# Row sums of a 32 x 512 x 1024 tensor: another assignment of rows to partitions, larger loads, another division of the work, and another tail

## The chip, the cores and the metric

The kernel runs on one core of a Trainium2 chip. The metric is the device time of one execution in microseconds (us). Every run here is fast, that is undisturbed, with a granted clock of 1.0 (the full speed). The span that the profile shows is about 1.8 us shorter than the time of the same execution. The groups of runs were taken on different chips, each group with runs of the kernel before beside it, so across groups the ratios are safer to compare than the times.

## The reference

```python
x: float32 [32, 512, 1024]          # 67.1 MB
reference(x) = np.sum(x, axis=-1)   # float32 [32, 512], 64 KB
```

A load is issued from the queue of one engine (SyncE, ScalarE or GpSimd) and is carried by 16 DMA engines in packets. In the records here a packet is one contiguous run for one partition: a 4 MB load of the kernel before is 128 packets of 32 KB.

The input is read once and one addition is made per element. So this is a question of how long the loads take, and of what is left to do before the first and after the last byte.

## The kernel before

The 16384 rows are cut into 16 tiles of 1024 rows. Each tile is one contiguous block of 4 MB. Partition p gets 8 consecutive rows of it, a run of 32 KB, so neighbouring partitions lie 32 KB apart in HBM. VectorE sums the even tiles with one instruction each, ScalarE the odd ones row by row. Results go out in nine stores, eight of them from the GpSimd queue.

```python
Q = 8; W = Q * dim
x_t = x.flatten_outer_dims().rearrange("(n p q) d -> n p (q d)", p=P, q=Q, n=ntiles)
out_v = out.rearrange("b s -> (b s)").rearrange("(n p q) -> p n q", p=P, q=Q, n=ntiles)
bounds = list(range(2, ntiles - 1, 2)) + [ntiles - 1, ntiles]
head_launchers = [nc.sync, nc.scalar] * 6
...
for i in range(ntiles):
    t = inpool.tile([P, W], fp32)                 # 5 buffers of 4 MB
    if i >= ntiles - 2:                           # last two tiles: four loads of 2 rows each
        ...  # last tile: nc.vector.tensor_reduce of 128 x 2 x 1024, four times
    elif i % 2 == 0:
        eng.dma_start(out=t, in_=x_t[i])
        nc.vector.tensor_reduce(out=dst, in_=t.rearrange("p (q d) -> p q d", q=Q), ...)
    else:
        ...  # nc.scalar.activation(Copy, accum_out=dst[:, q:q+1]), 8 rows
    if (i + 1) in bounds:
        ...  # a store of the finished sums: nc.gpsimd, the last one nc.sync
```

## Time and profile before

Time before: 165.77 us (three runs, 165.76 to 165.94). In the trace:

| | us |
|---|---|
| first load packet starts | 1.75 |
| last load packet ends | 159.03 |
| last reduction starts, ends | 159.47, 161.76 |
| last store issued, span ends | 161.78, 164.15 |

The page of the kernel before, parts 1 and 2: busy share of each compute engine, then the span in 40 slices with the busy tenths of the DMA engines and the bytes they moved.

```profile
DVE 74.5 (45%) x13; ACT 64.3 (39%) x121; POOL 5.9 (4%) x12
DMA  7899999998999989999999899999999998999960
GB/s 256 383 479 415 407 479 391 447 449 383 503 391 439 457 384 471 423 407 479 391 441 455 385 471 415 409 479 399 439 447 391 472 417 383 421 423 419 423 243 1
```

No compute engine is half busy, while the DMA engines are busy from the first slice to the last but one. The chain that ended last and the table of windows agree. The window columns are start and end, length, VectorE, ScalarE and GpSimd busy time (with instructions), clock, DMA share, GB/s.

```profile
DMA 86%; DVE 7%; ACT 5%; issue 0%; ACTq 0%; SPq 0%
...
40.00:80.00 40.00, 24.91 (x3) 16.85 (x32) 1.45 (x2) 1.00 1.00 429
80.00:120.00 40.00, 18.52 (x3) 11.12 (x21) 0.73 (x1) 1.00 1.00 432
```

The timeline shows what comes after the stream. Columns are start, length, engine, line, operation, and in brackets the idle time before it and what ended it.

```profile
159.47 2.29 DVE L59 TENSOR_REDUCE stage<-t 128x2 f32<-128x2048 f32 x1 [0.21 <-DMA t<-in_x_dram]
161.78 0.35 SPq L99 DMA_DIRECT2D out_dram<-stage  x1
```

The trace also has a record of every DMA packet. A 32 KB packet takes 1213 ns and an 8 KB packet 311 ns. Sixteen engines at one 32 KB packet per 1213 ns are 432 GB/s. The Trainium skill, "DMA: Bandwidth & Descriptors", section "Where 436 GB/s comes from", puts the ceiling of the SBUF ports at 435 GB/s. This trace stays just below it: its middle windows run at 429 to 432.

### The profile page before, as it was taken

To read this page: it belongs to the slowest core of one execution; us is meant where nothing else is said; L and a number is where in the kernel's file an instruction comes from. 1 tells how busy PE (TensorE), PEld (TensorE's weight loads), DVE (VectorE), ACT (ScalarE), POOL (GpSimd) and SP (SyncE) were. 2 spreads that over 40 slices of the span, in tenths; PEclk is the share of its full clock that TensorE was granted. 3 is DMA by queue.
4 is the path that set the end of the run, shared out by engine and by line. 5 is a ranking of instruction groups with operands and counts; after the bars stand their busy time and mean duration, and the time that the engine had idled before them with its cause. 6 is when DMAs were issued, how large, how long until landed. Compare 5 with 4: busy or idle time off the path is not lost.

```text
span 164.1 us, 241 instructions
## 1 busy us (share of the span) xinstructions
DVE 74.5 (45%) x13; ACT 64.3 (39%) x121; POOL 5.9 (4%) x12
## 2 busy tenths in 40 slices
DVE  0000049600794990039700892595008920055994
ACT  3000049600693000099101980000496006999940
POOL 0000000200001000000100001000001000010110
DMA  7899999998999989999999899999999998999960
GB/s 256 383 479 415 407 479 391 447 449 383 503 391 439 457 384 471 423 407 479 391 441 455 385 471 415 409 479 399 439 447 391 472 417 383 421 423 419 423 243 1
DMA packets 3569, 67.18 MB, mean 409 GB/s; under 512 B 640, under 2 KB 752, under 8 KB 752
## 3 DMA queue, kind: packets, MB, share of 16 engines
q1 hardware_dynamic: 2448, 41.95, 60.1%
q10 hardware_dynamic: 864, 25.17, 35.5%
q0 software_dynamic: 256, 0.06, 0.2%
q14 instruction: 1, 0.01, 0.0%
HBM read 67.11 MB, written 0.07 MB: 409 GB/s over the span
## 4 chain that ended last, share of the span: by engine, by line
DMA 86%; DVE 7%; ACT 5%; issue 0%; ACTq 0%; SPq 0%
DMA t<-in_x_dram 86%; DVE stage L78 5%; ACT sc L88 5%; DVE stage L59 1%; ACTq L85 0%; SPq L77 0%; SPq L85 0%; ACTq L88 0%
## 5 line engine op out<-in xcount | busy, mean ns | idle before, releaser
L88 ACT ACTIVATE sc<-t 128x1024 f32<-128x1024 f32 x56 | 58.3, 1041 | 91.7 <-DMA t<-in_x_dram 91.7
L78 DVE TENSOR_REDUCE stage<-t 128x8 f32<-128x8192 f32 x7 | 60.8, 8686 | 71.6 <-DMA t<-in_x_dram 71.6
L59 DVE TENSOR_REDUCE stage<-t 128x2 f32<-128x2048 f32 x6 | 13.7, 2286 | 15.6 <-DMA t<-in_x_dram 15.6
L99 POOL DMA_DIRECT2D out_dram<-stage x8 | 5.7, 718 | 152.3 <-ACT sc L88 98.8
L88 ACT ACTIVATION_READ_ACCUMULATOR sc<-t 128x1 f32 x56 | 10.4, 186 | 0.0
L70 ACT ACTIVATE sc<-t 128x1024 f32<-128x1024 f32 x4 | 4.2, 1039 | 0.0
L88 ACT ACT_TABLE_LOAD x1 | 1.3, 1283 | 1.7 <-PEq L114 1.7
L70 ACT ACTIVATION_READ_ACCUMULATOR sc<-t 128x1 f32 x4 | 0.7, 185 | 0.0
L114 POOL MEMSET const-float32-0.0<- 128x1 f32 x1 | 0.1, 99 | 0.2 <-issue 0.2
L114 POOL MEMSET const-bfloat16-1.0<- 128x1 bf16 x1 | 0.1, 102 | 0.0
L114 POOL MEMSET const-float32-1.0<- 128x1 f32 x1 | 0.1, 99 | 0.0
L114 POOL MEMSET const-uint8-127<- 128x1 uint8 x1 | 0.1, 99 | 0.0
## 6 DMA issues: line engine op xcount, KB each, us to landing
t<-in_x_dram SPq DMA_DIRECT2D x8, 4096.0 KB, 39.8
t<-in_x_dram ACTq DMA_DIRECT2D x6, 4096.0 KB, 31.0
t<-in_x_dram SPq DMA_DIRECT2D x8, 1024.0 KB, 27.5
out_dram<-stage POOLq DMA_DIRECT2D x7, 8.0 KB, 8.0
out_dram<-stage POOLq DMA_DIRECT2D x1, 4.0 KB, 1.7
out_dram<-stage SPq DMA_DIRECT2D x1, 4.0 KB, 1.4
```

The lines of the kernel that those rows point to most:

```text
L59: nc.vector.tensor_reduce(out=sdst, in_=t[:, s * QS * dim : (s + 1) * QS * dim].rearrange("p (q d) -> p q d", q=QS), axis=mybir.AxisListTy ...
L70: nc.scalar.activation(out=sc, in_=t[:, q * dim : (q + 1) * dim], func=mybir.ActivationFunctionType.Copy, accum_out=dst[:, q : q + 1],)
L78: nc.vector.tensor_reduce(out=dst, in_=t.rearrange("p (q d) -> p q d", q=Q), axis=mybir.AxisListType.X, op=mybir.AluOpType.add,)
L88: nc.scalar.activation(out=sc, in_=t[:, q * dim : (q + 1) * dim], func=mybir.ActivationFunctionType.Copy, accum_out=dst[:, q : q + 1],)
L99: oeng.dma_start(out=out_v[:, n0:n1], in_=src)
L114: nc = _bacc.Bacc("TRN2", target_bir_lowering=False, num_devices=1)
```

## The change

The intent: give each partition 128 consecutive rows, so that loads are 64 KB runs and the whole result is one store of 512 B per partition; issue everything from one queue; let VectorE do the bulk; and let the last pieces fall in size (8, 4, 2, 1 rows, then three cuts of one row) so that little work is left when the last byte lands.

```diff
-    x_t = x.flatten_outer_dims().rearrange("(n p q) d -> n p (q d)", p=P, q=Q, n=ntiles)
-    out_v = out.rearrange("b s -> (b s)").rearrange("(n p q) -> p n q", p=P, q=Q, n=ntiles)
+    J = rows // P                                   # 128
+    BIG = 16
+    x_v = x.flatten_outer_dims().rearrange("(p j) d -> p j d", p=P)
+    out_v = out.rearrange("b s -> (b s)").rearrange("(p j) -> p j", p=P)
+    nbig = J // BIG - 1                             # 7
+    tail = [(8, 4), (4, 2), (2, 1)]                 # rows, of which ScalarE takes
...
+        def rows_of(t, a, n, j, n_act):
+            nv = n - n_act
+            block = t[:, a * dim : (a + n) * dim].rearrange("p (n d) -> p n d", d=dim)
+            nc.sync.dma_start(out=block, in_=x_v[:, j : j + n, :])
+            if nv:
+                vec(sums[:, j : j + nv], block[:, :nv, :])
+            for q in range(nv, n):
+                act(sums[:, j + q : j + q + 1], block[:, q, :], dim)
+        for i in range(nbig):
+            t = inpool.tile([P, BIG * dim + 2], fp32)     # 3 buffers of 8 MB
+            rows_of(t, 0, BIG, i * BIG, BIG // 2 if i == nbig - 1 else 0)
+        t = inpool.tile([P, BIG * dim + 2], fp32)
+        a = 0
+        for n, n_act in tail:
+            rows_of(t, a, n, nbig * BIG + a, n_act)
+            a += n
+        rows_of(t, a, 1, nbig * BIG + a, 1)
...
+        cuts = [0, 384, 768, dim]
+        for c0, c1 in zip(cuts, cuts[1:]):
+            nc.sync.dma_start(out=last[:, c0:c1], in_=x_v[:, j, c0:c1])
+        for i, (c0, c1) in enumerate(zip(cuts, cuts[1:])):
+            if c1 < dim:
+                vec(last[:, dim + i : dim + i + 1], last[:, c0:c1])
+            else:
+                vec(sums[:, j : j + 1], last[:, c0 : dim + i])
+        nc.sync.dma_start(out=out_v, in_=sums)
```

With this row order neighbouring partitions lie 512 KB apart in HBM. That is the pitch.

More of the change, by code (lines that the diff above doesn't have):

```diff
@@ L17 @@
     fp32 = mybir.dt.float32
+    P = 128
     batch, seq, dim = x.shape
     rows = batch * seq
-    P = 128
-    Q = 8
-    W = Q * dim
-    ntiles = rows // (P * Q)
-    x_t = x.flatten_outer_dims().rearrange("(n p q) d -> n p (q d)", p=P, q=Q, n=ntiles)
-    out_v = out.rearrange("b s -> (b s)").rearrange("(n p q) -> p n q", p=P, q=Q, n=ntiles)
-    bounds = list(range(2, ntiles - 1, 2)) + [ntiles - 1, ntiles]
-    head_launchers = [nc.sync, nc.scalar] * 6
+    J = rows // P
+    BIG = 16
+    x_v = x.flatten_outer_dims().rearrange("(p j) d -> p j d", p=P)
@@ L33 @@
+    out_v = out.rearrange("b s -> (b s)").rearrange("(p j) -> p j", p=P)
+    nbig = J // BIG - 1
+    tail = [(8, 4), (4, 2), (2, 1)]
     with (
-        tc.tile_pool(name="in", bufs=5) as inpool,
-        tc.tile_pool(name="scratch", bufs=4) as spool,
+        tc.tile_pool(name="in", bufs=3) as inpool,
+        tc.tile_pool(name="scratch", bufs=1) as spool,
         tc.tile_pool(name="stage", bufs=1) as stpool,
     ):
-        stage = stpool.tile([P, ntiles * Q], fp32)
-        prev = 0
-        for i in range(ntiles):
-            t = inpool.tile([P, W], fp32)
-            eng = head_launchers[i] if i < len(head_launchers) else nc.sync
-            dst = stage[:, i * Q : (i + 1) * Q]
-            if i >= ntiles - 2:
-                NSUB = 4
-                QS = Q // NSUB
-                engs = (
-                    ["s", "v", "s", "v"] if i == ntiles - 2 else ["v", "v", "v", "v"]
-                )
-                for s in range(NSUB):
-                    nc.sync.dma_start(
-                        out=t[:, s * QS * dim : (s + 1) * QS * dim],
-                        in_=x_t[i][:, s * QS * dim : (s + 1) * QS * dim],
-                    )
-                for s in range(NSUB):
-                    sdst = dst[:, s * QS : (s + 1) * QS]
-                    if engs[s] == "v":
-                        nc.vector.tensor_reduce(
-                            out=sdst,
-                            in_=t[:, s * QS * dim : (s + 1) * QS * dim].rearrange(
-                                "p (q d) -> p q d", q=QS
-                            ),
-                            axis=mybir.AxisListType.X,
-                            op=mybir.AluOpType.add,
-                        )
-                    else:
-                        for q in range(s * QS, (s + 1) * QS):
-                            sc = spool.tile([P, dim], fp32)
-                            nc.scalar.activation(
-                                out=sc,
-                                in_=t[:, q * dim : (q + 1) * dim],
-                                func=mybir.ActivationFunctionType.Copy,
-                                accum_out=dst[:, q : q + 1],
-                            )
-            elif i % 2 == 0:
-                eng.dma_start(out=t, in_=x_t[i])
-                nc.vector.tensor_reduce(
-                    out=dst,
-                    in_=t.rearrange("p (q d) -> p q d", q=Q),
-                    axis=mybir.AxisListType.X,
-                    op=mybir.AluOpType.add,
-                )
-            else:
-                eng.dma_start(out=t, in_=x_t[i])
-                for q in range(Q):
-                    sc = spool.tile([P, dim], fp32)
-                    nc.scalar.activation(
-                        out=sc,
-                        in_=t[:, q * dim : (q + 1) * dim],
-                        func=mybir.ActivationFunctionType.Copy,
-                        accum_out=dst[:, q : q + 1],
-                    )
-            if (i + 1) in bounds:
-                n0, n1 = prev, i + 1
-                prev = i + 1
-                src = stage[:, n0 * Q : n1 * Q].rearrange("p (n q) -> p n q", q=Q)
-                oeng = nc.sync if n1 == ntiles else nc.gpsimd
-                oeng.dma_start(out=out_v[:, n0:n1], in_=src)
@@ new lines, with vec, act @@
+        sums = stpool.tile([P, J], fp32)
+        scratch = spool.tile([P, dim], fp32)
+        def vec(dst, src):
+            nc.vector.tensor_reduce(
+                out=dst, in_=src, axis=mybir.AxisListType.X, op=mybir.AluOpType.add
+            )
+        def act(dst, src, n):
+            nc.scalar.activation(
+                out=scratch[:, :n],
+                in_=src,
+                func=mybir.ActivationFunctionType.Copy,
+                accum_out=dst,
+            )
+        def rows_of(t, a, n, j, n_act):
[6 more added lines that the diff above has]
+                act(sums[:, j + q : j + q + 1], block[:, q, :], dim)
@@ new lines @@
+        for i in range(nbig):
[7 more added lines that the diff above has]
+        rows_of(t, a, 1, nbig * BIG + a, 1)
+        a += 1
+        j = nbig * BIG + a
+        last = t[:, a * dim :]
+        cuts = [0, 384, 768, dim]
+        for c0, c1 in zip(cuts, cuts[1:]):
+            nc.sync.dma_start(out=last[:, c0:c1], in_=x_v[:, j, c0:c1])
```

## The prediction

> **What bounds the kernel now.** The loads. The page's part 2 shows the DMA engines at 9 tenths in nearly every slice, and the table of windows shows DMA share 1.00 and 429 to 432 GB/s from 40 to 120 us, while VectorE is busy 45% and ScalarE 39% of the 164.1 us span. The chain of waits that ended last is 86% load. By the trace's packet records loads run from 1.75 to 159.03 us; the single engines finish between 158.0 and 159.03. A 32 KB packet takes 1213 ns (27.0 GB/s, times 16 = 432), an 8 KB packet 311 ns. From the two I estimate 9 ns per packet plus 0.0367 ns per byte: 435.5 GB/s without packet cost. That is the 435 GB/s fabric ceiling in the Trainium skill, "DMA: Bandwidth & Descriptors", section "Where 436 GB/s comes from". So the steady stream has under 1% to give.
>
> After it (chain, timeline): a 2.29 us reduction of 128x2048 from 159.47, store issued at 161.78, end of span 164.15.
>
> **What the change does.**
> 1. Bulk in 64 KB runs: half as many packets. Estimate: 56 fewer per engine at 9 ns, 0.5 us off the stream (0 if the hardware cuts them into 32 KB again).
> 2. The eight GpSimd stores go: 128 packets of about 28 ns and 128 semaphore writes of 9 ns on 16 engines, 0.3 us off the stream (queue 0: 0.2% of engine time).
> 3. The last reduction shrinks from 2048 to 258 elements per partition. From 8686 ns for 8192 and 2286 for 2048 (1.04 to 1.06 ns per element plus about 0.15 us) I estimate 0.4 us: 1.9 us off the end. Each falling piece needs less compute than the next takes to arrive.
> 4. One store of 64 KB, 512 B per partition, instead of the last one of 4 KB: its 8 packets per engine of 28 ns instead of 9 ns add about 0.15 us.
> 5. Off the critical path: VectorE gets the bulk, 16 x 1.09 = 17.4 us per 8 MB load that takes 19.4 us to arrive; three 8 MB buffers leave about 20 us of slack. One queue instead of two: the span 140 to 155 us already runs on one queue with DMA share 1.01.
> 6. The risk: consecutive rows per partition put the partitions 512 KB apart in HBM (before: 32 KB). The same skill page, "Latency and other measured facts", reports for copies 207 GB/s at a 512 KiB pitch against 214 full, and far less at 2 MiB. No trace here shows it yet. I take full rate as likeliest, with a loss up to 3% (4.7 us) as the minor case.
>
> **Sum.** -0.5 -0.3 -1.9 +0.15 = -2.55 us, to about 163.2; with some weight on the pitch and on uncut packets: 163.4 us (-1.4%). Range 162.2 to 166.8. Chances: faster by over 2% 0.14, within 2% 0.76, slower by over 2% 0.10.
>
> **What would show it.** Step 1: packets of 64 KB near 2.42 us, about 434 GB/s in the middle windows. Step 2: no GpSimd queue. Step 3: the last reduction under 0.5 us, and under 3.2 us from last load to end of span. Step 5: DMA share 1.00 throughout, VectorE about 70% busy. Step 6 wrong: packets of equal size taking visibly longer, or below 425 GB/s in the middle.
>
> **What would make it wrong.** A pitch effect on even some of the 16 engines (all must finish); small last pieces landing late; compute backlog at the end.

## The result, and the profile after

164.14 us (four runs, 164.04 to 164.34) against 165.80 us. The ratio is 0.9898, with a 95% interval of 0.9884 to 0.9912: 1.0% faster. A repeat in a later round gave 164.14 us and 0.9895.

The page after, the lines that answer to those before:

```profile
DVE 121.4 (75%) x13; ACT 19.7 (12%) x33; POOL 0.2 (0%) x4
DMA  7989979979969969979989998998998997998990
DMA 74%; DVE 22%; SPq 1%; issue 0%; DVEq 0%
```

VectorE does the bulk now and still has a quarter of its time free. The chain of waits passes through it ("DVE 22%") because a buffer comes free when VectorE has read it. This does not stop the stream: the next load's issue is released while two others are queued or in flight. In the timeline VectorE is idle for 2.1 to 2.3 us before each later bulk reduction, and the load issued at 118.07 begins only when the load ahead of it has ended, at 138.6 on the mean of the engines, about 20 us later:

```profile
100.82 17.22 DVE L41 TENSOR_REDUCE sums<-t 128x16 f32<-128x16384 f32 x1 [2.12 <-DMA t<-in_x_dram]
118.07 1.77 SPq L56 DMA_DIRECT2D t<-in_x_dram  x4
120.18 17.22 DVE L41 TENSOR_REDUCE sums<-t 128x16 f32<-128x16384 f32 x1 [2.14 <-DMA t<-in_x_dram]
```

The windows show the steady stream; a 64 KB packet counts in one window only, so two neighbouring windows must be read together, and their mean is 432 GB/s.

```profile
40.00:80.00 40.00, 34.76 (x3) 0.00 (x0) 0.00 (x0) 1.00 0.97 419
80.00:120.00 40.00, 34.44 (x2) 0.00 (x0) 0.00 (x0) 1.00 1.03 446
```

The timeline of the end:

```profile
158.51 1.01 DVE L41 TENSOR_REDUCE t<-t 128x1 f32<-128x384 f32 x2 [0.68 <-DMA t<-in_x_dram]
158.93 0.19 ACT L46 ACTIVATION_READ_ACCUMULATOR scratch<-t 128x1 f32 x1
159.56 0.42 DVE L41 TENSOR_REDUCE sums<-t 128x1 f32<-128x258 f32 x1
160.04 0.35 SPq L85 DMA_DIRECT2D out_dram<-sums  x1
```

The last reduction is 0.42 us instead of 2.29. But there is no idle time before it: VectorE works through three reductions in a row from 158.51 on.

The packet records side by side. The trace does not name the engine of a packet, but each of the 16 engines starts one of the first 16.

| | before | after |
|---|---|---|
| load packets per engine | 176 | 112 |
| usual time of a bulk packet | 1213 ns (32 KB) | 2418 ns (64 KB) |
| first packets of the 16 engines start | 1.75 to 2.87 us | 1.73 to 2.91 us |
| mean start of these | 1.96 us | 2.13 us |
| last load packet ends | 159.03 us | 158.77 us |
| from there to the end of the last reduction | 2.73 us | 1.21 us |
| from the store's issue to the end of the span | 2.37 us | 2.42 us |

So of the 1.68 us that the span lost, 1.52 came from the reductions at the end. The stream gave only 0.26 us, where the prediction had it give 0.8, and the store with its issue took 0.1 back. Two questions for the chip: why did the stream give so little, and why did the end give 1.5 and not 1.9?

### The profile page after: what moved, and what is told of

Its sections match the earlier page's. It is cut to its first block, busy times and chain, and to the rows that moved or that the text cites. A ratio compares the mean times of both kernels' runs of the same rounds, so it can differ in the third digit from the quotient of the medians.

```text
span 162.5 us, 119 instructions
## 1 busy us (share of the span) xinstructions
DVE 121.4 (75%) x13; ACT 19.7 (12%) x33; POOL 0.2 (0%) x4
## 4 chain that ended last, share of the span: by engine, by line
DMA 74%; DVE 22%; SPq 1%; issue 0%; DVEq 0%
DMA t<-in_x_dram 74%; DVE sums L41 21%; SPq L56 1%; DVE t L41 1%; DVEq L41 0%
## 5 line engine op out<-in xcount | busy, mean ns | idle before, releaser
L41 DVE TENSOR_REDUCE sums<-t 128x16 f32<-128x16384 f32 (+5 forms) x11 | 120.4, 10941 | 37.9 <-DMA t<-in_x_dram 37.9
L46 ACT ACTIVATE scratch<-t 128x1024 f32<-128x1024 f32 x16 | 16.9, 1057 | 138.7 <-DMA t<-in_x_dram 138.2
L46 ACT ACTIVATION_READ_ACCUMULATOR scratch<-t 128x1 f32 x16 | 3.0, 187 | 0.0
L41 DVE TENSOR_REDUCE t<-t 128x1 f32<-128x384 f32 x2 | 1.0, 548 | 0.7 <-DMA t<-in_x_dram 0.7
```

The source lines that it names most:

```text
L41: nc.vector.tensor_reduce(out=dst, in_=src, axis=mybir.AxisListType.X, op=mybir.AluOpType.add)
L46: nc.scalar.activation(out=scratch[:, :n], in_=src, func=mybir.ActivationFunctionType.Copy, accum_out=dst,)
```

## The experiments

Twelve runs. The theory at the start was that fewer packets, fewer stores and a shorter tail each give something and the new row order costs nothing. The rival was that the new order, with partitions 512 KB apart, takes part of it back. The prediction had named this with the skill's "DMA: Bandwidth & Descriptors", section "Latency and other measured facts": copies at a row pitch of 512 KiB ran at 207 GB/s instead of 214, and slower at larger powers of two.

### 1. The row order alone (b_rows)

The kernel before, with the new order only:

```diff
-    x_t = ...rearrange("(n p q) d -> n p (q d)", p=P, q=Q, n=ntiles)
-    out_v = ...rearrange("(n p q) -> p n q", p=P, q=Q, n=ntiles)
+    x_t = ...rearrange("(p n q) d -> n p (q d)", p=P, q=Q, n=ntiles)
+    out_v = ...rearrange("(p n q) -> p n q", p=P, q=Q, n=ntiles)
```

> The kernel before with only the row order of the change: each partition gets 128 consecutive rows, so partitions lie 512 KB apart in HBM instead of 32 KB; packets stay 32 KB, queues, stores and tail stay. Theory (the pitch costs nothing): 165.8 us within 0.2, 32 KB packets 1213 ns, the slow first packets as in the kernel before (1.6 to 2.1 us). Rival (the pitch eats part of the gain, at the head or in the stream): 166.2 us or more, and visibly longer packets.

Measured: 166.31 us (166.09 to 166.44) against 165.91; ratio 1.0026 (1.0014 to 1.0039). The row order alone costs 0.4 us, as the rival said. But not by longer packets: the median of a 32 KB packet is 1213 ns as before. The cost is at the start. The 16 engines' first packets end at 4.03 us on average instead of 3.75, and the latest of them at 4.65 instead of 4.08. The stream then ends 0.31 us later.

### 2. The stores (b_rows_onestore)

```diff
-    bounds = list(range(2, ntiles - 1, 2)) + [ntiles - 1, ntiles]
+    bounds = [ntiles]
```

> The same with one store of 64 KB at the end in place of the nine stores. Theory (the eight early stores take 0.3 us of the 16 engines' time, the larger last store gives 0.1 back): 0.2 us less than with the nine stores. Rival (the stores hide in the stream's gaps): no difference, or 0.1 us more.

Measured: 166.23 us (166.12 to 166.37), ratio 1.0021 (1.0008 to 1.0034): 0.08 us less than with nine stores, inside the spread of either. The last load packet ended at 159.36 us against 159.33. So the eight stores cost nothing that can be seen here, though the spread of the runs leaves room for the expected 0.2 us. Whether the stores ran beside load packets on the same engines is not shown: the records have 17 packets in flight on 16 engines for 5% of the time, but without the eight stores just as often.

### 3. The packet size (a_32k)

The changed kernel, each 64 KB run loaded as two of 32 KB:

```diff
-            nc.sync.dma_start(out=block, in_=x_v[:, j : j + n, :])
+            for h in range(0, n, 8):
+                k = min(8, n - h)
+                nc.sync.dma_start(out=block[:, h : h + k, :], in_=x_v[:, j + h : j + h + k, :])
```

> The changed kernel with every 64 KB run loaded as two of 32 KB, nothing else. Prediction's step 1: 0.5 us slower than the changed kernel (164.65). Theory now (packets of one engine overlap by about 3 ns, so a packet costs 5 to 6 ns): 0.3 us slower, 164.45. Rival (64 KB packets also make the head slower, first packets of 3.1 us on average): the head gives it back, 164.1 to 164.2, with first packets near 1.8 us.

Measured: 164.50 us (164.43 to 164.99), ratio 0.992 (0.9906 to 0.9933): 0.36 us slower than the changed kernel by the medians. The edit adds 56 packets per engine, so one packet costs 6.4 ns. The prediction had taken 9 ns from the packets' durations, but successive packets of one engine overlap by about 3 ns in the records. The 6.4 ns are rough: two of the five runs lie 0.3 to 0.6 us above the other three, and the interval overlaps that of the changed kernel (0.9884 to 0.9912), so the predicted 9 ns are not excluded.

### 4. The cuts of the last row (a_uncut)

```diff
-        cuts = [0, 384, 768, dim]
+        cuts = [0, dim]
```

> The changed kernel with the last row loaded in one piece of 4 KB and reduced at once (1024 elements, 1.2 us), instead of three cuts. Theory (the cuts arrive about 0.5 us apart and hide two of the three reductions only in part, as each takes 0.5 us): 0.4 us slower, 164.55. Rival (the cuts land together, so the chain of three is worth nothing): no difference, 164.1.

Measured: 164.42 us (164.36 to 164.51), ratio 0.9913 (0.9899 to 0.9926): about 0.3 us slower. The cuts are worth something, less than 0.4 us. The timeline of this variant:

```profile
158.71 1.22 DVE L41 TENSOR_REDUCE sums<-t 128x1 f32<-128x1024 f32 x1 [1.30 <-DMA t<-in_x_dram]
160.00 0.35 SPq L85 DMA_DIRECT2D out_dram<-sums  x1
```

Here VectorE waits 1.30 us for the last landing, which comes 0.48 us after the last packet's end (158.23), and starts at once. In the changed kernel the last packet ended at 158.77. Where a last reduction waited for its data, it started 0.44 us (kernel before) to 0.56 us (a_head_pair, section 7) after the last packet's end. By that the last cut had landed at 159.2 to 159.3, an estimate from these numbers, and its reduction began at 159.56. So VectorE was late by 0.2 to 0.35 us with its own two earlier cuts.

### 5. The changed kernel again, and its repeat under the old row order (after_again, a_blocks)

> The changed kernel once more, word for word, as the yardstick for the others of this call: 164.1 us, the 16 engines' first 64 KB packets ended at 5.23 us on average. The first profile showed about 0.4 us of lengthened packets between 20 and 60 us; if that is chance, this profile need not show it.

The repeat, unedited, gave 164.14 us (164.04 to 164.39), ratio 0.9895. Its profile does not have the 0.4 us of longer packets that the first one showed between 20 and 60 us; nor was the first profile's execution the fastest (164.25 against 164.04). That episode is chance. Its cause is not known.

```diff
-    x_v = x.flatten_outer_dims().rearrange("(p j) d -> p j d", p=P)
-    out_v = out.rearrange("b s -> (b s)").rearrange("(p j) -> p j", p=P)
+    x_b = x.flatten_outer_dims().rearrange("(n p q) d -> n p q d", p=P, q=BIG)
+    out_v = out.rearrange("b s -> (b s)").rearrange("(n p q) -> p n q", p=P, q=BIG)
```

> The changed kernel with the old row order: each 8 MB load is one contiguous block, partitions 64 KB apart instead of 512 KB. Theory (a far pitch costs about 0.28 us, at the start of the stream only, as between the kernel before and its variant with the new rows: mean end of the first packets 3.75 and 4.03 us): first packets end 0.28 us earlier on average, about 4.95 us, packets 2418 ns as before; the store now has 1024 pieces of 64 B, about 0.4 us more at the end, so the time stays near 164.1 to 164.3. Rival (the late head is due to 64 KB packets or to the single queue): first packets end at 5.2 us and the time rises to 164.5.

Measured: 164.38 us (164.21 to 164.50), ratio 0.9904 (0.9889 to 0.9919). The first packets end at 5.04 us on average (5.27 in the repeat of the changed kernel) and the latest at 5.41 (5.91). The stream ends at 158.05 us against 158.60, 0.55 us earlier. The store, now 1024 pieces of 64 B, gives this back: it lands 2.2 us after its issue instead of 1.5.

### 6. A pitch of 448 KB, and a contiguous first load (a_448, a_head)

2048 rows are one contiguous block (partitions 64 KB apart); of the other 14336 each partition gets 112 consecutive ones. The block's sums are stored early, from ScalarE's queue. In a_head the block is loaded first, in a_448 second.

```diff
+    H = P * BIG
+    x_h = xf[0:H].rearrange("(p j) d -> p j d", p=P)
+    x_r = xf[H:rows].rearrange("(p j) d -> p j d", p=P)
...
-        for i in range(nbig):
+        for i in [1, 0] + list(range(2, nbig)):        # a_448; in a_head range(nbig)
...
+            if i == 0:
+                nc.scalar.dma_start(out=out_h, in_=sums[:, :BIG])
...
-        nc.sync.dma_start(out=out_v, in_=sums)
+        nc.sync.dma_start(out=out_r, in_=sums[:, BIG:])
```

> The changed kernel with 112 consecutive rows per partition (partitions 448 KB apart, not a power of two); the other 2048 rows are one contiguous block, loaded second and stored early from the ScalarE queue. If the head's cost comes from the power of two in the pitch: first packets end 0.28 us earlier (4.95) and the time is 163.8. If it comes from any far pitch: first packets at 5.2 us and 164.1 us.

> The same with the contiguous block loaded first. Both theories of the pitch: first packets end at about 4.95 us, and the time falls by 0.25 us against the changed kernel, to 163.85. Rival (the head has nothing to do with pitch): 164.1 us.

Measured: a_448 163.46 us (163.45 to 163.92), ratio 0.9856 (0.9841 to 0.9872); a_head 163.45 us (163.38 to 163.52), ratio 0.9849 (0.9834 to 0.9864). Both are 0.7 us faster than the changed kernel in the same rounds, more than either theory said.

| | pitch at start | mean end of first packets | latest of them | last load packet ends |
|---|---|---|---|---|
| after_again | 512 KB | 5.27 us | 5.91 us | 158.60 us |
| a_blocks | 64 KB | 5.04 | 5.41 | 158.05 |
| a_448 | 448 KB | 5.02 | 5.42 | 158.06 |
| a_head | 64 KB | 5.02 | 5.31 | 157.96 |

The distance itself is harmless: 448 KB starts as well as 64 KB does. It is 512 KB that starts late, and its latest engine is worse off than its mean. This is not one unlucky profile: in the four profiles with 64 KB packets and a 512 KB pitch (the changed kernel, after_again, a_uncut, a_tail2048) the latest first packet ends at 5.72 to 5.91 us, in a_blocks, a_448, a_head and a_head_pair (section 7) at 5.31 to 5.49. The usual 64 KB packet takes 2418 ns in all four of the table. The latest first packet accounts for 0.5 to 0.6 us of the 0.54 to 0.64 us in the end of the stream. My expectation had used the mean, 0.25 us; but every load waits for its slowest engine, and the lateness is kept. In the records each load closes with 16 packets of 4 B, as many as there are engines. The latest of them comes 0.61 us behind their mean after the first load of after_again, and still 0.61 us after the tenth, 133 us later; in a_blocks it is 0.38 and 0.37, in a_448 0.40 and 0.39, in a_head 0.29 and 0.30. The gap does not shrink, as it would if other engines took over work from the late one. The rest of the 0.7 us, under 0.1, lies in the reductions and in the last store, which is 56 KB here.

The timeline of a_448, as that of the changed kernel but 0.73 us earlier:

```profile
157.78 1.01 DVE L49 TENSOR_REDUCE t<-t 128x1 f32<-128x384 f32 x2 [0.66 <-DMA t<-in_x_dram]
158.82 0.42 DVE L49 TENSOR_REDUCE sums<-t 128x1 f32<-128x258 f32 x1
159.31 0.35 SPq L95 DMA_DIRECT2D out_dram<-sums  x1
```

### 7. Attempts to better it (a_head_pair, a_head_2q, a_head_2q_pair)

On top of a_head: the last two rows together in three cuts, VectorE summing one row and ScalarE the other (pair), and the first load halved over two queues (2q).

```diff
 # pair: t is laid out as 2 x 512 | 2 x 256 | 2 sums | 2 x 256 | 2 sums
+        parts = [(0, 512, o), (512, 768, o + 1024), (768, dim, o + 1538)]
...
+            nc.sync.dma_start(out=t[:, at : at + 2 * w]..., in_=x_r[:, j - BIG : j - BIG + 2, c0:c1])
...
+                vec(t[:, o + 1536 + i : o + 1537 + i], t[:, at : at + w])
+                act(t[:, o + 2050 + i : o + 2051 + i], t[:, at + w : at + 2 * w], w)
...                                               # the last cut, with the two sums before it
 # 2q: the first load
+                nc.sync.dma_start(out=block[:, :h, :], in_=src_of(0, h))
+                nc.scalar.dma_start(out=block[:, h:, :], in_=src_of(h, n - h))
```

> The block-first version with another tail: the last two rows come together in three cuts (512, 256, 256 columns of both), VectorE sums the one row, ScalarE the other. Theory (in the changed kernel VectorE works off the three cuts of the last row one after the other and ends about 0.3 us later than the last landing plus one short reduction needs): 0.2 us less, 163.25 us, the last reductions start within 0.1 us of the last landing. Rival (the ScalarE path with its separate readout of the accumulator is as slow as the chain on VectorE): no difference, 163.45.

> The block-first version with its first load split over two queues (8 rows each from SyncE and ScalarE), as the kernel before starts. Theory (the late start of the changed kernel came from the pitch, not from the single queue): at most 0.1 us less, 163.35 to 163.45. Rival (the single queue starts the engines later): 0.2 us less or more, 163.2.

> Both together, the best version so far by these reasons: 163.15 to 163.25 us, against 165.9 of the kernel before 1.6% less.

Measured: 163.51 us (0.9855), 163.54 us (0.9857) and 163.59 us (0.9858), each with an interval of about 0.0015 either way, against 163.45 (0.9849) for a_head. None is better. The timeline of a_head_pair:

```profile
158.85 0.42 ACT L54 ACTIVATE scratch<-t 128x258 f32<-128x258 f32 x1
158.86 0.42 DVE L49 TENSOR_REDUCE sums<-t 128x1 f32<-128x258 f32 x1 [0.31 <-DMA t<-in_x_dram]
159.18 0.19 ACT L54 ACTIVATION_READ_ACCUMULATOR scratch<-t 128x1 f32 x1
```

The tail did what it should: VectorE now waits 0.31 us for the last landing, and from the last packet's end (158.30) to the end of the reductions pass 1.07 us instead of 1.21. But the stream ended 0.33 us later than in a_head. About half of this, 0.17 us, was there after the first load already, where the two kernels do the same, so it is chance of the start. The rest fits the packets: the three paired cuts make 48 packets per engine where the four small loads that they replace made 32, and the records give these 2.98 us per engine instead of 2.74. So the small packets cost about what the shorter chain gave. That the second queue gave nothing agrees with the skill's "DMA: Bandwidth & Descriptors", section "Issuing engines are not separate DMA queues", which lets a second queue save only issue time.

### 8. The old end on the changed kernel (a_tail2048)

```diff
-        rows_of(t, a, 1, nbig * BIG + a, 1)
-        ...  # and the three cuts of the last row
+        rows_of(t, a, 2, nbig * BIG + a, 0)
```

> The changed kernel with its last two rows loaded as one piece and summed by one reduction of 2048 elements on VectorE, as the kernel before ends; all else as changed. Prediction's step 3 (1.9 us for the shorter last reduction): 166.0 us. Theory now (the end of the last load to the end of the last reduction is 2.73 us in the kernel before and 1.21 in the changed one, 1.5 us; the tail here has 32 fewer small packets per engine at 6 to 9 ns, 0.2 to 0.25 us back): 1.25 us slower than the changed kernel, 165.4 us.

Measured: 165.45 us (165.40 to 165.60), ratio 0.9973 (0.9959 to 0.9986): 1.3 us slower than the changed kernel. Its timeline ends as that of the kernel before:

```profile
158.71 2.29 DVE L41 TENSOR_REDUCE sums<-t 128x2 f32<-128x2048 f32 x1 [1.24 <-DMA t<-in_x_dram]
161.07 0.35 SPq L74 DMA_DIRECT2D out_dram<-sums  x1
```

The last pieces of less than two rows are therefore most of what the change brought (the pieces of 8, 4 and 2 rows stay in this variant). The change without them would be within 0.3% of the kernel before. (The text on record says 32 fewer packets per engine; by the records it is 24: 88 against 112.)

## Why the prediction was right or wrong

The measured time, 164.14 us, lies in the stated range and in the class "within 2%". The point was 163.4 us, 0.74 us too low, and the sum behind it, -2.55 us, was too large by 0.9 us. The range of 162.2 to 166.8 us, nearly three times as wide as the gain, was wide enough to hold this. The prediction's own test of the end failed: it wanted under 3.2 us from the last load to the end of the span, and 3.70 were measured. Its list of what would make it wrong had named both causes, a pitch effect on some of the engines and a backlog of compute at the end, but the sum held neither; the pitch got some weight in the point alone. Term by term:

| term | predicted | measured | from |
|---|---|---|---|
| 1. fewer packets | -0.5 | -0.4 (rough) | a_32k: 6.4 ns per packet, 64 fewer per engine |
| 2. and 4. stores | -0.15 | -0.1 (not clear of zero) | b_rows_onestore |
| 3. shorter last reduction | -1.9 | -1.5 | traces: 2.73 and 1.21 us after the last packet; a_tail2048 agrees |
| 6. row order | 0 (some weight on a loss) | +0.4 (+0.7 in the changed kernel) | b_rows (a_448, a_head) |
| sum | -2.55 | -1.6 | measured by the medians -1.66 |

- **What bounds the kernel: right.** The stream stays at 432 GB/s, and every variant's time followed the start of the stream, its packets and what came after its last byte. VectorE at 75% is off the path, as step 5 said.
- **Step 1: right in kind, perhaps a little too large.** 64 KB packets take 2418 ns, as expected (2.42 us). The cost of a packet was taken from durations that overlap; the measured 6.4 ns and the 9 ns are not apart beyond the noise.
- **Step 2: probably mis-sized.** 0.3 us of engine time for the stores was read as 0.3 us of stream time. b_rows_onestore shows no such loss: its stream ended 0.03 us later than with the nine stores. The times alone do not exclude it.
- **Step 3: the size of the last reduction was right (0.42 us against 0.4), the gain was not.** "Each falling piece needs less compute than the next takes to arrive" fails for the last cuts. Two reductions of 384 elements take 1.01 us and the last cut is only 256 elements, so VectorE reaches it late. The sign of it is the missing idle time before the last reduction. This cost 0.2 to 0.35 us, most of the 0.4 that was missing; a_head_pair, where the wait is back, confirms the reading, though it pays for it in packets.
- **Step 6: taken as the minor case, and it is a term of the sum.** The check that I had named, longer packets or a lower rate in the middle, would have missed it: both are unchanged. The cost is in the first packets of the 16 engines, and the latest one carries it to the end. Removing the 512 KB pitch from the changed kernel gave 0.7 us, adding it to the kernel before cost 0.4 us.

The terms add up to -1.6 against -1.66 us, but each has an uncertainty of 0.1 to 0.3 us, and with the 0.7 us that the row order cost in the changed kernel they would give -1.3, so the close agreement is partly luck. Left open: why 512 KB starts later than 448 or 64 KB. No run here looks inside HBM. The skill's entry offers aliasing of channels as an inference; the finding that 448 KB is free of it fits that, and does not prove it. Why the pitch cost 0.4 us in one kernel and 0.7 in the other is answered in part by the closing packets. In the kernel before the latest one comes 0.33 us behind the mean after the first load, but 0.56 us in the last nine loads: it loses most of its even start by itself, between 90 and 138 us, and b_rows (0.59 and 0.63) has less left to lose. Why it does so is open.

## What to carry to other kernels

When a stream is at its limit, look at its two ends, and reckon at the start with the slowest engine and not with the mean: rows that put the partitions 512 KB apart cost 0.4 to 0.7 us here, and 448 KB cost nothing. Make the last pieces small, but add up the reductions that follow one another on one engine after the last landings, and the packets (some 6 ns each per engine by a_32k) that smaller pieces add. The best version here, a_head, keeps the falling pieces and the 64 KB loads, takes a contiguous block first and avoids the 512 KB pitch: 163.45 us, 1.5% below the kernel before and 0.4% below the change. a_448, with the block second, is as good (163.46 us), so it is the avoided pitch that counts and not the place of the block.

## What the Trainium skill lacked or had wrong

- "DMA: Bandwidth & Descriptors", "Latency and other measured facts", the entry on row pitches: it gives rates of copies. For loads alone at 512 KB the steady packets are not slower (2418 ns at 512, 448 and 64 KB). The loss is at the start: the latest first packet ends at 5.9 us instead of 5.3 to 5.4, and the time is 0.4 to 0.7 us longer. 64 KB is a power of two as well, and harmless.
- The same section gives about 0.6 us to the first byte for loads from the sync and scalar queues. Here the first load is issued at 0.73 us, the first engine's first packet starts at 1.73 and the last engine's at 2.91. The spread over the engines is in no page.
- The same page speaks of the cost of a packet for small ones only; it has no time per packet for large packets of such loads. Here 56 more per engine cost 0.36 us, 6.4 ns each (rough, see section 3); 8, 32 and 64 KB packets take 309 to 313, 1213 to 1214 and 2418 ns.
- The same page, "Anatomy of one DMA", gives about 2 us fixed cost per transfer on the GpSimd path, mostly the receipt; it has no such breakdown for the sync queue. For these loads into SBUF a reduction that waited started 0.44 to 0.56 us after the last packet's end, and the 64 KB store to HBM lands 1.5 us after its issue.
